# Summing the adaLN partial sums over the partitions on GpSimd instead of on the tensor engine

## The chip, the cores and the metric

The kernel runs on one core of a Trainium2 chip. The metric is the device time of one execution in microseconds, the median over several executions. Engine names are those of the profile: PE is the tensor engine (PEld its weight loads), DVE the vector engine, ACT the scalar engine, POOL is GpSimd, and SP is the queue that issues the loads.

## What is computed

The reference is two layers of a transformer-like block for 256 latent tokens and 256 context tokens of width 1024, in float32. Each layer has a mixer (two attentions and a pooling mixer in parallel, merged by gates) and a channel mixer (an MLP of width 4096). Both are modulated: a vector `c` per stream (one for the latents, one for the context) gives six rows of 1024 numbers per layer, a shift, a scale and a gate for each of the two sub-layers. The change touches the way in which these rows are computed.

```python
def adaln(v, w, b):
    m = jax.nn.silu(v) @ w + b
    return jnp.split(m, 6, axis=-1)

for l in range(DEPTH):
    sh1, sc1, g1, sh2, sc2, g2 = adaln(c, w_ada[l], b_ada[l])       # and the same with c_ctx
    h = rmsnorm(x, norm1[l]) * (1 + sc1) + sh1
    x = x + g1 * merge(...)(h)
    x = x + g2 * mlp(rmsnorm(x, norm2[l]) * (1 + sc2) + sh2, ...)
```

## The kernel before

The program is written out by cooperative threads under a planner (`_Flow`). Each engine has an estimate of its own time table (`_Engine`, line 78; PE in `_TensorEngine`), with a fixed cost and a cost per column for every instruction. A thread yields a time, an event or nothing, and the planner issues instructions in the order in which the engines should run them by these estimates. The order of every engine's queue is thus fixed when the program is built. On the chip each engine takes its queue in order and waits on semaphores where an input is late.

PE multiplies float32 values as pairs (a rounded part `hi` and a rest `lo`), three matmuls for each product (`mm3`, line 433). A weight piece of 128x1024 is loaded by SP into `st` (line 350), cast to `wh` by ACT and split into `wl` by DVE (`halves`, line 366). Four such pairs are in use at most (W_HL_BUFS), and loads run three pieces ahead.

The adaLN rows of the first norm of layer 0 are made on PE at the start (`First`, line 517). All others come later, beside the main work, in the thread `ada_all` (line 1757), at a low priority. For each half of a row (512 columns) `ada_acc` (line 564) loads the 1024x512 block of w_ada in four pieces and adds up silu(c) times the rows on DVE. The result is a tile `acc` of 128x512 for each stream, whose 128 partitions still have to be summed. There are 32 such tiles. They end in one of two ways:

- `ada_cols_end` (line 602), 20 tiles, for shift and scale. These are wanted as columns, with the features on the partitions. PE transposes the four 128x128 blocks into a PSUM bank, DVE reduces each block along its columns to one number a partition and adds the bias column. Both instructions are issued on DVE's queue in their planned order. When both of shift and scale are there, `finish_mod` makes the norm's factor. The tiles belong to norm 2 of layer 0 (8), norm 1 of layer 1 (8), norm 2 of layer 1 (4, the latents alone), in this order.
- `ada_rows_end` (line 637), 12 tiles, for the gates. These are wanted as rows on every partition. ACT and DVE split `acc` into a pair, PE multiplies it by a matrix that is filled with 0.5 or 1.0 (`ones`, lines 676 to 682), and DVE adds the bias row `grow`, which was loaded to all partitions. The factor 0.5 belongs to the first gate of each layer. The order is: first gate of layer 0 (4 tiles), second gate of layer 0 (4), first gate of layer 1 (2), second gate of layer 1 (2). `to_residual` (line 1479) multiplies the matmul's result by the row.

Both ends wait ADA_SLACK (10 us by the planner's clock, line 44) before the PE work, and take PSUM banks only where two stay free. `calm_way` (line 248) keeps this work away from the norms.

POOL does little: constants at the start, the power -1/2 in the norms (`norm_tile`, line 725) and in the normalisation of keys and queries (`qk_norm`, line 900, by `rms_scale`, line 706), the tables `tab`, and small memsets. For keys, DVE's product `z` reads the power's result at once.

Of the kernel before, what the change touches and what calls it, by code (L numbers as in the profile page):

```python
# [15 lines left out]
P = 128  # L16
# [15 lines left out]
B_BUFS = 64  # L32
# [11 lines left out]
ADA_SLACK = 10.0  # L44
# [7 lines left out]
# order in which the layers take the chunks of w_in (see _layout)  # L52
# [6 lines left out]
# the loads of the start: token tiles, halves of the first norm's shift and scale, halves of the first chunks  # L59
# [11 lines left out]
class _Event:  # L71
    """A point of the program whose results other threads wait for."""
# [5 lines left out]
class _Engine:  # L78
    """An engine whose instructions advance the flow's estimate of its time table."""
# [14 lines left out]
    def calm(self, slack):  # L94
        """wait until the engine's queue is short"""
        while self._end > self._f.now + slack:
            yield self._end - slack

    def __getattr__(self, op):
        fn = getattr(self._e, op)  # L100

        def call(*args, **kw):
# [9 lines left out]
            if kw.get("op") == ALU.pow:  # L112
                per, cost = 0.09, 0.37
            if self._sb and any(p.space == bass.MemoryType.SB for p in ins[:1]):
                cost += self._sb
# [22 lines left out]
class _TensorEngine:  # L138
# [6 lines left out]
    def _step(self, out, lhsT, rhs, size, transpose=False):  # L145
        """the array's clock is full in a tick after one with enough columns, else half"""
# [27 lines left out]
class _Flow:  # L174
    """Cooperative threads that emit the program in the order in which the tensor engine should run it.

    A thread yields None (it can go on at once), a time (it can go on then) or an event."""
# [26 lines left out]
    def ready(self, *aps, eng=None):  # L204
        """when an engine sees the last write to these regions"""
        got = 0.0
        for ap in aps:
            for b in self._blocks(ap):
                t, e, late = self.times.get(b, (0.0, None, 0.0))
                got = max(got, t if e is eng else t + late)  # L210
        return got
# [15 lines left out]
    def held(self, pool):  # L227
        """how many tiles of a pool are in use"""
        p = self.pools[pool]
        p[1] = [t for t in p[1] if t > self.now]  # L230
        return p[0] + len(p[1])

    def free(self, *aps):
        """the last uses of these tiles are in the program"""
# [8 lines left out]
    def room(self, pool, n, most):  # L243
        """wait until n more tiles of a pool fit"""
# [3 lines left out]
    def calm_way(self):  # L248
        """wait while any norm is on its way"""
# [39 lines left out]
# priorities of the threads, the lowest number first  # L289
# [4 lines left out]
def kernel(ctx: ExitStack, tc: tile.TileContext, a: dict, out: bass.AP):  # L294
# [55 lines left out]
    def stage(src, nk, ncol):  # L350
        """a load of at most 1024 columns, on its way"""
# [14 lines left out]
    def halves(v, nk, ncol):  # L366
        """(hi, lo) of a staged load's rows"""
# [13 lines left out]
    class Chunk:  # L381
        """the (hi, lo) pairs of a chunk's rows, in two pieces"""
# [12 lines left out]
        def used(self, k):  # L395
            """row k is not needed any more, nor are those before"""
# [3 lines left out]
    class Stream:  # L400
        """Chunks of weights [128, nk, ncol], each staged in two loads and split ahead of its use"""
# [24 lines left out]
        def next(self):  # L426
            """the next chunk"""
# [5 lines left out]
    def mm3(ps, lh, rh, start, stop):  # L433
        """ps (+)= (lh_hi + lh_lo)^T (rh_hi + rh_lo), without lo * lo"""
# [13 lines left out]
    class Pair:  # L448
        """a (hi, lo) pair of tiles that some thread is going to write"""
# [19 lines left out]
    def reload_x():  # L469
        """the stream's input for the first residual sum"""  # L470
# [14 lines left out]
    # silu(c) as columns: 0.5 c (1 + tanh(c / 2))  # L485
# [9 lines left out]
    # adds the (hi, lo) rows of both vectors  # L495
# [14 lines left out]
    def finish_mod(l, which, vec, half):  # L510
        """A = norm (1 + scale), B = shift as per-partition columns"""
# [5 lines left out]
    class First:  # L517
        """half of the columns of shift and scale of layer 0, norm 1, both vectors, on the tensor engine"""
# [6 lines left out]
        def row(self, typ, kk, w):  # L525
            """one of the eight row tiles of one type: rows (hi, lo) x vectors"""
# [37 lines left out]
    def ada_acc(l, j, vecs, accs):  # L564
        """per-partition partial sums of silu(c) @ w_ada[:, 512 j : 512 j + 512]"""
# [27 lines left out]
    def ada_cols(l, which, vecs):  # L593
        """shift and scale columns of norm `which`"""
# [6 lines left out]

    def ada_cols_end(l, which, vecs, half, typ, accs, left):
        idx = 3 * which + typ
        c0 = idx * 8 + half * 4
        yield fl.now + ADA_SLACK
        for acc, vec in zip(accs, vecs):
            yield from banks(1, 2)
            pt = bank("act")
            for i in range(4):
                PE.transpose(pt[:, i * P : (i + 1) * P], acc[:, i * P : (i + 1) * P], ident)  # L610
            yield fl.ready(pt)
            dst = mods[l][:, 2 * which + typ, vec, half * 4 : half * 4 + 4]
            V.tensor_reduce(out=dst, in_=pt.rearrange("p (i q) -> p i q", i=4), axis=AX.X, op=ALU.add)
            yield fl.ready(dst)
            V.tensor_tensor(out=dst, in0=dst, in1=b_col[:, l, c0 : c0 + 4], op=ALU.add)
            free(acc, pt)
# [12 lines left out]
    def ada_rows(l, idx, vecs, ones, factor):  # L629
        """factor * gate rows on every partition: rows[l, idx][vec][half]"""  # L630
        left = [0, 1]
        for half in range(2):
            accs = []
            yield from ada_acc(l, idx * 2 + half, vecs, accs)
            fl.spawn(ada_rows_end(l, idx, vecs, ones, factor, half, accs, left), P_ADA)

    def ada_rows_end(l, idx, vecs, ones, factor, half, accs, left):
# [8 lines left out]
        hl = []  # L646
        yield from fl.room("b", 2 * len(accs), B_BUFS - ADA_SPARE)
        for acc in accs:
            yield from fl.calm_way()
            ah, al = tmp(F32R, "ach"), tmp(F32R, "acl")  # L650
            yield from hilo_steps(acc, ah, al)
            hl.append((ah, al))
            free(acc)
        yield fl.ready(*[q for p in hl for q in p]) + ADA_SLACK
        for (ah, al), vec, g in zip(hl, vecs, gs):
            yield from banks(1, 2)
            ps = bank("ar")
            PE.matmul(ps, ones, ah, start=True, stop=False)
            PE.matmul(ps, ones, al, start=False, stop=True)
            free(ah, al)  # L660
            yield fl.ready(g, ps)
            yield from fl.calm_way()
            V.scalar_tensor_tensor(out=g, in0=g, scalar=factor, in1=ps, op0=ALU.mult, op1=ALU.add)
            free(ps)
# [9 lines left out]
    identr = const([P, P], F32R, "identr")  # L674
    S.copy(out=identr, in_=ident)
    ones = {}
    for f in (0.5, 1.0):
        of = half(s="ones")
        G.memset(of[:, :P], f)
        ones[f] = const([P, P], F32R, f"ones{f}")  # L680
        S.copy(out=ones[f], in_=of[:, :P])
        free(of)
# [23 lines left out]
    def rms_scale(ss, n, width):  # L706
        """(ss / width + eps) ** -0.5 in place"""
# [4 lines left out]
    class Normed:  # L712
        """hi and lo tiles of a modulated norm, features on partitions"""
# [11 lines left out]
    def norm_tile(l, which, t, xh):  # L725
        """x * rstd of one token tile"""
# [57 lines left out]
    def mod_out(l, which, hT, stream, k, v, cols, ev, by, ps, left):  # L784
        """a feature tile of the modulated norm"""
# [24 lines left out]
    def norm_by_tile(l, which, hT, t):  # L810
        """one token tile of the modulated norm of stream 0"""
# [36 lines left out]
    def layer(l, hT, hT_next):  # L848
# [6 lines left out]
        def pair(s):  # L855
            """(hi, lo) of NQ columns"""
# [5 lines left out]
        def duo(dt, s):  # L862
            """a tile of NQ columns"""
# [9 lines left out]
        # rope tables with the gains folded in: T[kind][:, 0] -> y0, T[kind][:, 1] -> y1  # L873
# [26 lines left out]
        def qk_norm(ps, c0, nh, kind, t, hi, lo, ev, rs=None):  # L900
            """heads ps[:, c0 : c0 + 64 nh], rotated, to hi and lo [P, nh, ..., 64]; normalised, or (queries) with the
            norm's factor times SCALE in rs"""
# [66 lines left out]
        def done_with(ps):  # L969
            """one of the threads that read this bank has read it"""  # L970
# [947 lines left out]
```

## Time and profile before

| | before |
|---|---|
| median of 3 executions | 1159.73 us (1159.59 to 1160.59) |
| the profiled execution, span from first to last instruction | 1159.7 us |
| mean granted clock of PE | 0.994 |
| busy: PE, DVE, ACT, POOL | 1138.5, 872.7, 636.2, 70.7 us |
| instructions: PE matmuls, DVE, ACT, POOL | 6636, 1653, 1356, 84 |

No time of the profiled execution other than its span is on the page; it agrees with the median to 0.1 us. Busy time counts an engine's own work. PE's matmuls overlap at their ends, so the start-to-start distance tells more of what one costs than its duration. The chain of the page follows the work that ended last backwards, and names for each step what it waited for.

### The profile page before, as it was taken

The numbers are of one execution on the slowest core, as the hardware profiler recorded it, in microseconds if no ns is written. First come the engines' busy times: TensorE is split into PE (matmuls) and PEld (weight loads), VectorE is DVE, ScalarE is ACT, GpSimd is POOL, SyncE is SP. The second block draws the span as 40 slices with busy tenths as digits, with TensorE's granted clock in tenths as the row PEclk, the third lists the DMA queues.
The fourth block names the chain that finished last, engine by engine and source line by source line (L and its number), as shares of the span: only waits on it lengthen the run. The fifth ranks groups of instructions, "written<-read, shape, count | busy, mean of one in ns | idle before, by whom it ended". The sixth has DMA issues, their size and how long they took to land.

```text
span 1159.7 us, 17946 instructions
## 1 busy us (share of the span) xinstructions
PE 1138.5 (98%) x6636; PEld 998.0 (86%) x6636; DVE 872.7 (75%) x1653; ACT 636.2 (55%) x1356; POOL 70.7 (6%) x84
## 2 busy tenths in 40 slices
PE   5999999999999999999999999989999999999998
PEld 2898889888888898888888888889999998999886
DVE  5878989889888679878677634689777885987453
ACT  6867786664633564321133323576877865666332
POOL 0224001100000000000000000023002000000000
PEclk9899999999999999999999999999999999999999
DMA  8752235243435435556655423554334471775562
GB/s 308 271 166 97 85 105 188 90 153 121 136 137 178 138 119 178 180 180 214 213 178 185 163 92 107 166 168 153 103 128 137 155 241 40 269 238 183 192 216 75
DMA packets 59992, 186.85 MB, mean 161 GB/s; under 512 B 7296, under 2 KB 8064, under 8 KB 59904
## 3 DMA queue, kind: packets, MB, share of 16 engines
q1 hardware_dynamic: 59904, 185.71, 47.8%
q8 instruction: 52, 0.85, 0.3%
q14 instruction: 36, 0.29, 0.1%
HBM read 184.63 MB, written 1.05 MB: 160 GB/s over the span
## 4 chain that ended last, share of the span: by engine, by line
PE 95%; DMA 2%; ACT 2%; DVE 1%; SPq 0%; issue 0%; POOL 0%; DVEq 0%; POOLq 0%
PE tm L167 28%; PE h L167 23%; PE g L167 17%; PE qkv L167 8%; PE br L167 6%; PE sc L167 3%; PE po L167 2%; PE pT L171 2%; PE u L167 1%; DMA ad<-in_wada_dram 1%; PE xT L171 1%; PE ada L167 1%; PE act L171 1%; PE qT L171 1%; PE kT L171 1%; ACT hh L133 1%
## 5 line engine op out<-in xcount | busy, mean ns | idle before, releaser
L133 DVE TENSOR_TENSOR wl<-st,wh 128x1024 fp32r<-128x1024 f32 x216 | 263.6, 1223 | 133.7 <-ACT wh L133 133.1
L133 ACT CAST wh<-st 128x1024 fp32r<-128x1024 f32 x216 | 227.9, 1058 | 231.8 <-PE tm L167 151.2
L167 PE MATMUL h<-hh,wh 128*128 128x256 f32 (+1 forms) x736 | 186.7, 316 | 0.0
L167 PE MATMUL h<-hh,wl 128*128 128x256 f32 (+1 forms) x512 | 168.8, 330 | 0.2 <-DVE wl L133 0.2
L133 DVE SCALAR_TENSOR_TENSOR acc<-sta,s_col,acc 128x512 f32<-128x512 f32 x224 | 159.3, 743 | 3.0 <-DMA sta<-in_wada_dram 2.4
L167 PE MATMUL tm<-wh,ah 128*128 128x512 f32 x384 | 150.3, 391 | 0.0
L167 PE MATMUL tm<-wl,ah 128*128 128x512 f32 x384 | 149.5, 389 | 0.0
L167 PE MATMUL tm<-wh,al 128*128 128x512 f32 x384 | 149.5, 389 | 0.0
L167 PE MATMUL g<-hh,wh 128*128 128x512 f32 (+1 forms) x384 | 132.6, 345 | 0.0
L167 PEld LDWEIGHTS h<-hh,wh 128*128 128x128 f32 x736 | 124.1, 190 | 8.8
L167 PE MATMUL g<-hl,wh 128*128 128x512 f32 (+1 forms) x384 | 129.3, 337 | 0.0
L167 PE MATMUL g<-hh,wl 128*128 128x512 f32 (+1 forms) x384 | 129.3, 337 | 0.0
L167 PE MATMUL h<-hl,wh 128*128 128x512 f32 (+1 forms) x288 | 105.4, 366 | 0.1
L167 PEld LDWEIGHTS h<-hh,wl 128*128 128x128 f32 x512 | 97.0, 190 | 9.3 <-DVE wl L133 0.5
L167 PEld LDWEIGHTS tm<-wh,al 128*128 128x128 f32 x384 | 72.1, 188 | 15.2
L167 PEld LDWEIGHTS tm<-wl,ah 128*128 128x128 f32 x384 | 72.1, 188 | 14.7
L167 PEld LDWEIGHTS tm<-wh,ah 128*128 128x128 f32 x384 | 72.1, 188 | 14.5
L167 PE MATMUL qkv<-wh,hh 128*128 128x256 f32 x272 | 79.7, 293 | 1.1 <-ACT hh L133 1.1
L167 PE MATMUL qkv<-wl,hh 128*128 128x256 f32 x272 | 79.0, 290 | 1.8 <-DVE wl L133 1.8
L167 PEld LDWEIGHTS g<-hh,wl 128*128 128x128 f32 x384 | 72.8, 190 | 8.0
L167 PE MATMUL qkv<-wh,hl 128*128 128x256 f32 x272 | 79.1, 291 | 0.1
L167 PEld LDWEIGHTS g<-hh,wh 128*128 128x128 f32 x384 | 72.8, 190 | 6.7 <-ACT p L133 0.3
(188 smaller groups left out, 2178.6 us busy)
## 6 DMA issues: line engine op xcount, KB each, us to landing
st<-in_w_dram SPq DMA_DIRECT2D x136, 512.0 KB, 4.5
sta<-in_wada_dram SPq DMA_DIRECT2D x80, 512.0 KB, 4.1
st<-in_win_dram SPq DMA_DIRECT2D x72, 512.0 KB, 4.6
ad<-in_wada_dram SPq DMA_DIRECT2D x32, 256.0 KB, 7.1
st<-in_wout_dram SPq DMA_DIRECT2D x8, 512.0 KB, 5.5
wor<-in_wout_dram SPq DMA_DIRECT2D x16, 256.0 KB, 4.9
grow<-in_b_ada_dram SPq DMA_DIRECT2D x12, 256.0 KB, 5.1
kr<-in_wbr_a_dram SPq DMA_DIRECT2D x12, 256.0 KB, 5.0
```

The lines of the kernel that those rows point to most:

```text
L133: return fn(*args, **kw)
L167: return self._e.matmul(out, lhsT, rhs, start=start, stop=stop)
L171: return self._e.transpose(out, in_, identity)
```

## The change

Each partial sum is added up over the partitions by one `partition_all_reduce` on POOL, which leaves the sum on every partition (`ada_sum`, new). For the gates POOL then adds the bias row. For shift and scale POOL multiplies the sum by the identity, block by block, into the tile of the partial sum, and DVE reduces the result along its columns as before, now from SBUF. The ones matrices, the splits of the gates' partial sums, the transposes and ADA_SLACK are gone. The factor 0.5 of the first gates moves into the residual's product. The planner books 0.4 us and 6.3 ns a column for the all-reduce. The rest of the diff takes out comments.

```diff
+from concourse.bass_isa import ReduceOp
...
-ADA_SLACK = 10.0
...
+            if op == "partition_all_reduce":
+                per, cost = 6.3e-3, 0.4
...
+    def ada_sum(acc):
+
+        yield fl.ready(acc)
+        yield from fl.calm_way()
+        yield from fl.room("b", 1, B_BUFS - ADA_SPARE)
+        tot = tmp(s="tot")
+        G.partition_all_reduce(tot, acc, P, ReduceOp.add)
+        yield fl.ready(tot)
+        return tot
+
     def ada_cols_end(l, which, vecs, half, typ, accs, left):
...
-        yield fl.now + ADA_SLACK
         for acc, vec in zip(accs, vecs):
-            yield from banks(1, 2)
-            pt = bank("act")
-            for i in range(4):
-                PE.transpose(pt[:, i * P : (i + 1) * P], acc[:, i * P : (i + 1) * P], ident)
-            yield fl.ready(pt)
+            tot = yield from ada_sum(acc)
+
+            dg = acc.rearrange("p (i q) -> p i q", i=4)
+            G.tensor_tensor(out=dg, in0=tot.rearrange("p (i q) -> p i q", i=4), in1=ident.unsqueeze(1).to_broadcast([P, 4, P]), op=ALU.mult)
+            free(tot)
+            yield fl.ready(acc)
+            yield from V.calm(ADA_CALM[l])
             dst = mods[l][:, 2 * which + typ, vec, half * 4 : half * 4 + 4]
-            V.tensor_reduce(out=dst, in_=pt.rearrange("p (i q) -> p i q", i=4), axis=AX.X, op=ALU.add)
+            V.tensor_reduce(out=dst, in_=dg, axis=AX.X, op=ALU.add)
...
-        hl = []
-        yield from fl.room("b", 2 * len(accs), B_BUFS - ADA_SPARE)
-        for acc in accs:
-            yield from fl.calm_way()
-            ah, al = tmp(F32R, "ach"), tmp(F32R, "acl")
-            yield from hilo_steps(acc, ah, al)
-            hl.append((ah, al))
+        for acc, vec, g in zip(accs, vecs, gs):
+            tot = yield from ada_sum(acc)
             free(acc)
-        yield fl.ready(*[q for p in hl for q in p]) + ADA_SLACK
-        for (ah, al), vec, g in zip(hl, vecs, gs):
-            yield from banks(1, 2)
-            ps = bank("ar")
-            PE.matmul(ps, ones, ah, start=True, stop=False)
-            PE.matmul(ps, ones, al, start=False, stop=True)
-            free(ah, al)
-            yield fl.ready(g, ps)
-            yield from fl.calm_way()
-            V.scalar_tensor_tensor(out=g, in0=g, scalar=factor, in1=ps, op0=ALU.mult, op1=ALU.add)
-            free(ps)
+            yield fl.ready(g)
+            G.tensor_tensor(out=g, in0=g, in1=tot, op=ALU.add)
+            free(tot)
             rows[l, idx][vec][half] = g
...
-                V.tensor_tensor(out=tm[:, c], in0=rows[l, idx][t // 2][n][:, c], in1=ps[:, c], op=ALU.mult)
+                row = rows[l, idx][t // 2][n][:, c]
+                if idx == 2:
+
+                    V.scalar_tensor_tensor(out=tm[:, c], in0=row, scalar=0.5, in1=ps[:, c], op0=ALU.mult, op1=ALU.mult)
+                else:
+                    V.tensor_tensor(out=tm[:, c], in0=row, in1=ps[:, c], op=ALU.mult)
```

## Rows read from the trace of the kernel before

**Rows 1.** The page, busy time of each engine, share of the span and instructions.
```profile
PE 1138.5 (98%) x6636; PEld 998.0 (86%) x6636; DVE 872.7 (75%) x1653; ACT 636.2 (55%) x1356; POOL 70.7 (6%) x84
```
**Rows 2.** The chain that ended last: its shares by engine, then by line.
```profile
PE 95%; DMA 2%; ACT 2%; DVE 1%; SPq 0%; issue 0%; POOL 0%; DVEq 0%; POOLq 0%
...
by line: PE tm L167 28.0%; PE h L167 22.6%; PE g L167 17.1%; PE qkv L167 7.7%; PE br L167 5.8%; PE sc L167 2.6%; PE po L167 2.4%; PE pT L171 2.2%; PE u L167 1.4%; DMA ad<-in_wada_dram 1.2%; PE xT L171 0.9%; PE ada L167 0.8%; PE act L171 0.8
```
**Rows 3.** Busy time by stage: us from:to, length, busy time (instructions), clock, DMA share, GB/s.
```profile
178.00:354.00 176.00, 176.00 (x980) 152.34 (x979) 152.25 (x326) 98.86 (x248) 7.96 (x8) 1.00 0.40 134
...
402.00:625.00 223.00, 222.92 (x1097) 188.09 (x1096) 176.43 (x266) 79.01 (x108) 2.94 (x2) 1.00 0.54 181
...
745.00:800.00 55.00, 51.92 (x362) 48.75 (x361) 45.41 (x117) 41.09 (x126) 18.55 (x20) 0.97 0.52 168
```
**Rows 4.** Tile act: count, ns min/median/max, first and last start us, forms.
```profile
L171 PE MATMUL act<-ident,acc x80: 270/272/273, 231.8 to 620.6; 128*128 128x128 f32 x80
L133 DVE TENSOR_REDUCE mod<-act x20: 673/682/687, 233.3 to 623.2; 128x4 f32<-128x512 f32 x20
```
**Rows 5.** Groups of instructions (busy us, mean ns, idle before); last, tile res (as rows 4).
```profile
L133 DVE SCALAR_TENSOR_TENSOR grow<-grow,ar 128x512 f32<-128x512 f32 x12 | 8.1, 676 | 0.0
L133 DVE TENSOR_TENSOR acl<-acc,ach 128x512 fp32r<-128x512 f32 x12 | 8.1, 678 | 0.0
...
L133 DVE TENSOR_TENSOR res<-grow,tm x33: 414/686/689, 362.6 to 1155.9; 128x512 f32<-128x512 f32 x31, 128x256 f32<-128x256 f32 x2
```
**Rows 6.** PE's timeline around one tile's transposes and one ones-matmul: start us, us, instruction.
```profile
231.78 0.60 PE L171 MATMUL act<-ident,acc 128*128 128x128 f32 x4
232.13 0.48 PE L167 MATMUL g<-hh,wh 128*128 128x512 f32 x1
232.45 0.40 PE L167 MATMUL g<-hl,wh 128*128 128x512 f32 x1
...
146.08 0.39 PE L167 MATMUL ar<-ach,ones0.5_108 128*128 128x512 f32 x1
146.31 0.39 PE L167 MATMUL ar<-acl,ones0.5_108 128*128 128x512 f32 x1
```
**Rows 7.** Groups of POOL's instructions, shapes kept apart.
```profile
L133 POOL TENSOR_TENSOR tab<-rope,gains 128x256 f32<-128x256 f32 x8 | 8.5, 1088 | 1.0 <-DMA gains<-in_gains_dram 1.0
```
**Rows 8.** POOL's timeline at the start of the kernel and of layer 1.
```profile
1.01 0.29 POOL masks.py:199 TENSOR_SCALAR_AFFINE_SELECT ident<-ident 128x128 f32<-128x128 f32 x1
1.39 0.19 POOL L133 TENSOR_TENSOR pair_sum<-ident 128x2 f32<-128x2 f32 x1
...
785.08 1.01 POOL L133 TENSOR_TENSOR rsqA<-rsqA,neg_half 128x4 f32<-128x4 f32 x1 [2.08 <-DVE y L133]
786.05 0.70 POOL L133 TENSOR_TENSOR qr<-qr,neg_half 128x2 f32<-128x2 f32 x1
```
**Rows 9.** ACT's table load; loads by size: count, KB each, us to landing.
```profile
L133 ACT ACT_TABLE_LOAD x1 | 1.3, 1283 | 0.7 <-PEq L1907 0.7
...
ad<-in_wada_dram SPq DMA_DIRECT2D x32, 256.0 KB, 7.1
...
sink<-in_sink_dram SPq DMA_DIRECT2D x1, 6.0 KB, 6.0
pscale<-in_pscale_dram SPq DMA_DIRECT2D x1, 2.0 KB, 5.4
```
**Rows 10.** DVE's timeline: partial sums that end, and the product of the keys.
```profile
121.98 1.40 DVE L133 SCALAR_TENSOR_TENSOR acc<-sta,s_col,acc 128x512 f32<-128x512 f32 x2
...
167.25 1.41 DVE L133 SCALAR_TENSOR_TENSOR acc<-sta,s_col,acc 128x512 f32<-128x512 f32 x2
...
180.56 0.29 DVE L133 TENSOR_TENSOR z<-qkv,qr 128x128 f32<-128x128 f32 x1 [0.68 <-POOL qr L133]
```
**Rows 11.** Tiles qr and wl, their durations as in rows 4.
```profile
L133 POOL TENSOR_TENSOR qr<-qr,neg_half x16: 695/698/1693, 64.8 to 862.3; 128x2 f32<-128x2 f32 x16
L133 DVE TENSOR_TENSOR wl<-st,wh x216: 1203/1224/1755, 24.5 to 1145.7; 128x1024 fp32r<-128x1024 f32 x108
```

More of the change, by code (lines that the diff above doesn't have):

```diff
@@ L604, in ada_cols_end @@
         c0 = idx * 8 + half * 4
-        yield fl.now + ADA_SLACK
         for acc, vec in zip(accs, vecs):
-            yield from banks(1, 2)
-            pt = bank("act")
-            for i in range(4):
-                PE.transpose(pt[:, i * P : (i + 1) * P], acc[:, i * P : (i + 1) * P], ident)
-            yield fl.ready(pt)
+            tot = yield from ada_sum(acc)
[4 more added lines that the diff above has]
+            yield from V.calm(ADA_CALM[l])
             dst = mods[l][:, 2 * which + typ, vec, half * 4 : half * 4 + 4]
-            V.tensor_reduce(out=dst, in_=pt.rearrange("p (i q) -> p i q", i=4), axis=AX.X, op=ALU.add)
+            V.tensor_reduce(out=dst, in_=dg, axis=AX.X, op=ALU.add)
             yield fl.ready(dst)
             V.tensor_tensor(out=dst, in0=dst, in1=b_col[:, l, c0 : c0 + 4], op=ALU.add)
-            free(acc, pt)
+            free(acc)
         left.pop()
@@ L627, with ada_rows @@
             rows_ev[l, i] = _Event()
-    def ada_rows(l, idx, vecs, ones, factor):
+    def ada_rows(l, idx, vecs):
         left = [0, 1]
@@ L634, in ada_rows, with ada_rows_end @@
             yield from ada_acc(l, idx * 2 + half, vecs, accs)
-            fl.spawn(ada_rows_end(l, idx, vecs, ones, factor, half, accs, left), P_ADA)
-    def ada_rows_end(l, idx, vecs, ones, factor, half, accs, left):
+            fl.spawn(ada_rows_end(l, idx, vecs, half, accs, left), P_ADA)
+    def ada_rows_end(l, idx, vecs, half, accs, left):
         yield from fl.room("grow", len(vecs), GROW_BUFS)
@@ L675 @@
     S.copy(out=identr, in_=ident)
[L676 to L682, printed above, removed]
     rope = const([P, 2, 2, HD], F32, "rope")
@@ L1758, in ada_all @@
         yield layer_started[0]
-        yield from ada_rows(0, 2, (0, 1), ones[0.5], 0.5)
+        yield from ada_rows(0, 2, (0, 1))
         yield from ada_cols(0, 1, (0, 1))
-        yield from ada_rows(0, 5, (0, 1), ones[1.0], 1.0)
+        yield from ada_rows(0, 5, (0, 1))
         yield from ada_cols(1, 0, (0, 1))
         yield from ada_cols(1, 1, (0,))
-        yield from ada_rows(1, 2, (0,), ones[0.5], 0.5)
+        yield from ada_rows(1, 2, (0,))
         yield mlp_started[1]
-        yield from ada_rows(1, 5, (0,), ones[1.0], 1.0)
+        yield from ada_rows(1, 5, (0,))
     layer_started = [_Event()]
```

## The prediction

> **What bounds the kernel now.** I read the page first, then the chain, the groups of instructions, the timelines of POOL, DVE and PE, and last the busy time by stage. The page says that the tensor engine sets the time: PE is busy for 1138.5 of 1159.7 us, DVE for 872.7 and POOL for 70.7 [rows 1]. The chain agrees: 95% of it is PE, and the transposes of the partial sums alone (PE act) stand in it with 0.8%, some 9 us [rows 2]. The profiled execution has a span of 1159.7 us; the median of the runs is 1159.73, so I sum against 1159.7 and add nothing.
>
> The engine next to PE is DVE, and its room differs by stage. From 178 to 354 us it is busy for 152.25 of 176, from 402 to 625 us for 176.43 of 223 [rows 3]. All 20 reduces of a partial sum into a column lie in these two stretches, 233.3 to 623.2 us [rows 4]. DVE also splits every weight piece (216 `wl`) and takes its instructions in order, so a DVE instruction that waits holds the weights back.
>
> **What goes.** On PE, 80 transposes and 24 ones-matmuls, two for each of the 12 `grow` [rows 4, 5]. Four transposes start at 231.78 and the second matmul behind them at 232.45, where a matmul alone takes 0.23 [rows 6]: 0.67 - 0.23 = 0.44 us a tile, times 20 is 8.8 us. A ones-matmul starts 0.23 us after the one before it [rows 6]: 24 x 0.23 = 5.6. Together 14.4 us, all of it on the bound. DVE loses 12 `acl` of 0.678 and 12 `grow` of 0.676, 16.2 us [rows 5]; ACT loses 12 casts `ach`. Both leave slack only. Gone as well are 32 uses of a PSUM bank and the 10 us of ADA_SLACK.
>
> **What costs nothing.** The halving moves into the residual: a SCALAR_TENSOR_TENSOR in place of a TENSOR_TENSOR, 0.676 (as `grow` has it) against 0.686 us at 128x512 [rows 5]. The 12 bias loads stay on SP's queue in number and size. The two ones tiles (two memsets, two casts) lie under the loads of the start.
>
> **What comes.** POOL gets 32 partition_all_reduce, 20 products with the identity and 12 adds. An elementwise pass over 128x256 takes 1.088 us there [rows 7], so one over 128x512 about 2. The all-reduce has no row. From below: one such pass, 2 us. From above: the dearest POOL work by column, the power, takes 1.01 us for four columns and 0.70 for two [rows 7, 8], 0.155 a column, 80 us for 512. I take 3.6, nearer to the lower end because the power computes much per element and a sum does not; it is also what the planner books (0.4 + 512 x 6.3 ns). In this sum its length delays nobody, since the planner places the readers behind it.
>
> The term that decides is one that the planner doesn't book: **the change of program on POOL**. The diff names the all-reduce's sum from another module (`ReduceOp` of `bass_isa`) than the ALU operations that POOL's other calls use. In the trace POOL goes from memset to select to elementwise in 0.4 us [rows 8], so those sit together. Nothing shows that the all-reduce sits with them. If it doesn't, each step from all-reduce to elementwise and back needs the other code first. Call the price s. Nearest rows: ACT's one table load, 1.28 us [rows 9], for the lower end; 7.1 us, the slowest kind of load [rows 9], twice (two fetches in a row) for the upper, 14.2. I take 7.1: code must come from memory, and even 2 and 6 KB took 5.4 and 6.0 us to land in the busy part [rows 9]. The Trainium skill's GPSIMD Engine Reference (Instruction dispatch) says that the first call to a freshly loaded POOL kernel pays about 6 us that no instruction in the profile shows. No row here shows it; by that figure, as an estimate, the sum below gives 1277 us.
>
> Who waits? In ada_cols_end each tile is an all-reduce and then a product on POOL, and then a reduce on DVE, which is issued when the planner holds the product done. The swap before the first all-reduce hides in POOL's idle time; the one before its product does not (s late), nor do the two of the second vector (2s). So 3s = 21.3 us of DVE standing still for a pair of tiles, s = 7.1 for a single one. Behind the reduce stand `wl` and the softmax's reduces.
> - 178 to 354 us: four pairs, 85.2 us. DVE has 176 - 152.25 = 23.75 free and gets 1.4 back; 60 us too many.
> - 402 to 625 us: four pairs and four singles, 113.6 us. Free 46.6, got back 5.4; 61.6 too many.
> - A power for layer 0's keys stands in POOL's queue behind the pair of tiles finished at 169, and DVE's `z` at 180.56 waited 0.68 for it [rows 10]; now 3s = 21.3 more.
> - 745 to 800 us: the two tiles of layer 1's first gate fall among a row of powers [rows 8]: 4s = 28.4, of which I take half, 14.2, for the path, since DVE is busy for 45.41 of 55 there [rows 3].
> - The second gate of layer 1 ends near 1050 and is first used after 1068: nothing.
> - Where DVE is the bound, PE's savings don't count. What counts are the 16 ones-matmuls outside 402 to 625 us: -3.7.
>
> Sum: 60 + 61.6 + 21.3 + 14.2 - 3.7 = 153.4; 1159.7 + 153.4 = **1313 us**. With every wait on PE's path at s = 7.1 it is 85.2 + 113.6 + 21.3 + 28.4 - 14.4 = 234, 1394 us; with s = 4 it is 23 + 12 + 12 + 8 - 3.7 = 51, 1211; with s = 10 and every wait exposed 1475. Below s = 2.4 or so the room on DVE takes the waits and the change wins.
>
> **Rivals.**
> 1. *No swap: the all-reduce is one more POOL operation.* Then the new POOL work (32 x 3.6 + 32 x 2 = 180 us) lies on an engine busy for 6%, and 14.4 us leave the bound: 1145 to 1150 us. For it: the chain, and POOL's idle time. Against: nothing here shows both kinds resident. Chance 0.11.
> 2. *The all-reduce itself is slow* and POOL becomes the bound: at the upper end, 32 x 80 = 2560 us. The sum crosses at some 8 us apiece, when DVE's waits use up its room; at 30 us, 28 tiles need 840 us where some 500 lie between the first finished sum at 123 [rows 10] and 625, and the kernel is near 1159.7 + 840 - 500 = 1500. For it: the power's price per column. Against: a sum is not a power. The Trainium skill's GPSIMD Engine Reference (Cross-partition — where GPSIMD wins) gives 247.7 us for a partition-axis reduce of 128x2048. By that, as an estimate, a tile takes 62 us and the kernel over 2000; it is another instruction, and no row here shows either. Chance 0.05.
> 3. *No swap, but POOL and DVE get in each other's way.* The power over two columns took 0.70 alone and 1.69 at worst where DVE was full, and `wl` 1.22 at the median and 1.76 at worst [rows 11]: they hinder each other somewhere. If DVE stood still for all of the new POOL work, 8 x 5.6 = 45 us against 25 free in the first stretch and 16 x 5.6 = 90 against 52 in the second give +20 + 38 - 3.7, 1214 us. Against: DVE's usual times beside POOL are the plain ones. Chance 0.04.
> 4. *The PE time saved turns into other waits*: no change. The chain has 95% PE, so hardly; 0.02.
>
> **How the numbers follow.** The forecast has the rest, 0.78, and its time is the sum, 1313. Its own range is s = 4 to s = 10 exposed, 1211 to 1475; I set 1210 to 1490, which also takes in rival 3 and part of 2, and leaves out rival 1 and the slower end of rival 2. Measurement tells 0.2%, 2.3 us, from no change. Faster 0.11 (rival 1), same 0.02, slower 0.87.
>
> **What would show it.** POOL's timeline: gaps of s between each all-reduce and the elementwise instruction behind it, with nothing in them. The waits: DVE `mod` <- POOL at the head of the list, with about 8 and 15 us for the tiles of a pair, and PE and ACT waiting on DVE `wl`. PE busy well under 98% from 178 to 625 us, unchanged after 800. The forecast is wrong if POOL goes from all-reduce to product within a microsecond: then rival 1, or 2 if the all-reduce's own record is tens of us long. If the gaps are there and the time is still under 1200, DVE's waits had more cover than its free time.

## The result, and the profile after

The changed kernel takes **1358.75 us** (median of 4 executions, 1356.91 to 1361.71) against 1159.66 us of the kernel before, run beside it: a ratio of 1.1717, 95% interval 1.1701 to 1.1734. It is 199 us slower. The forecast was 1313 us, with 1210 to 1490 for the range: right sign, in the range, 46 us low.

First the page of the changed kernel (it answers to [rows 1, 2]): busy time by engine, two of the sliced rows (busy tenths of PE, PE's granted clock) and the chain's shares.

```profile
PE 1167.8 (86%) x6532; PEld 1011.2 (75%) x6532; DVE 890.3 (66%) x1629; ACT 629.1 (46%) x1342; POOL 227.1 (17%) x146
...
PE   6999998588598999076478799999689999999998
...
PEclk8999999789798999678688899999989999999999
...
PE 60%; issue 13%; DVE 11%; POOL 7%; ACT 5%; DMA 3%; SPq 0%; POOLq 0%; DVEq 0%; ACTq 0%
```

No engine is full any more. PE has 104 instructions fewer and yet is busy for 29 us longer, because the clock that it was granted fell (0.928 on the mean, 0.994 before), and the chain has lost its 95% of PE to waits. POOL is at 17%, so it is not a matter of throughput. POOL's timeline around one pair of partial sums shows what fills the time:

```profile
226.37 3.25 POOL L135 PARTITION_ALL_REDUCE tot<-acc  x1 [6.02 <-PE g L169]
236.73 1.28 POOL L135 TENSOR_TENSOR acc<-tot,ident 128x512 f32<-128x512 f32 x1 [7.11 <-issue]
244.05 3.25 POOL L135 PARTITION_ALL_REDUCE tot<-acc  x1 [6.04 <-PE g L169]
254.22 1.25 POOL L135 TENSOR_TENSOR acc<-tot,ident 128x512 f32<-128x512 f32 x1 [6.93 <-issue]
```

Between an all-reduce and the product behind it lie 7.1 and 6.9 us, put down to "issue": nothing that the profile shows was waited for. On the way back it is 6.0 (the releaser named there, PE, is only the nearest event; the gap is as long wherever the pattern stands). DVE takes its reduces in order, so it stands for these gaps; the timeline of DVE for the same pair, and the list of waits:

```profile
238.04 0.69 DVE L135 TENSOR_REDUCE mod<-acc 128x4 f32<-128x512 f32 x1 [3.96 <-POOL acc L135]
...
255.51 0.69 DVE L135 TENSOR_REDUCE mod<-acc 128x4 f32<-128x512 f32 x1 [13.40 <-POOL acc L135]
```
```profile
DVE mod L135 <- POOL acc L135: 198.1, 19, 37.1
...
POOL acc L135 <- issue: 122.0, 17, 7.9
...
PE h L169 <- DVE wl L135: 52.0, 5, 40.3
...
PE tm L169 <- DVE wl L135: 45.3, 8, 14.5
...
DVE z L135 <- POOL qr L135: 31.8, 5, 15.7
```

The 20 reduces wait 198.1 us in all (times and longest follow the sum), and behind them the weight splits `wl`, for which PE waits.

Where in the kernel is the time? The table has the length of five stretches in the profiled execution of every version that was run: to the first matmul of w_out; from there to the first power of layer 0's second norm; layer 0's MLP, up to the first power of layer 1's first norm; layer 1's mixer, up to its second norm; the rest. The experiments are explained below.

| version | us | ratio (95%) | mixer 0 | w_out 0 | MLP 0 | mixer 1 | rest |
|---|---|---|---|---|---|---|---|
| before | 1159.7 | 1 | 354.3 | 32.6 | 350.8 | 225.4 | 196.7 |
| after | 1358.8 | 1.1717 (1.1701-1.1734) | 410.2 | 42.0 | 464.4 | 244.2 | 195.8 |
| no_swap | 1183.7 | 1.0192 (1.0172-1.0211) | 356.7 | 36.4 | 361.2 | 233.2 | 195.8 |
| planner_knows | 1319.4 | 1.1366 (1.1344-1.1388) | 374.1 | 35.4 | 467.9 | 243.1 | 196.3 |
| knows_late_free | 1201.3 | 1.0360 (1.0344-1.0376) | 372.4 | 34.8 | 347.2 | 246.1 | 195.8 |
| dve_product | 1182.0 | 1.0181 (1.0162-1.0200) | 354.5 | 32.6 | 345.4 | 250.1 | 195.8 |
| dve_knows | 1178.3 | 1.0140 (1.0114-1.0166) | 357.8 | 32.5 | 345.2 | 245.4 | 195.8 |
| dve_early | 1160.1 | 0.9997 (0.9988-1.0006) | 361.0 | 33.2 | 343.6 | 223.5 | 196.2 |
| cols_on_pool | 1302.1 | 1.1218 (1.1200-1.1235) | 399.8 | 47.1 | 428.2 | 225.3 | 196.7 |
| rows_on_pool | 1192.1 | 1.0272 (1.0257-1.0288) | 366.7 | 32.6 | 349.1 | 249.6 | 195.8 |
| before_pool_load | 1246.9 | 1.0744 (1.0725-1.0763) | 386.7 | 32.5 | 395.8 | 226.7 | 202.5 |
| before_swaps | 1217.3 | 1.0505 (1.0484-1.0526) | 366.9 | 34.4 | 374.9 | 244.0 | 200.7 |
| before_sums | 1205.5 | 1.0382 (1.0367-1.0398) | 372.4 | 32.6 | 370.8 | 226.9 | 200.8 |
| **hybrid** | **1154.5** | **0.9949 (0.9937-0.9962)** | 354.7 | 32.5 | 343.6 | 225.8 | 195.8 |

(Span of the profiled execution before: 1159.7; after: 1356.6; the stretches add up to the spans.) The change loses 55.9 us in mixer 0, 9.4 in w_out, 113.6 in MLP 0 and 18.8 in mixer 1. In the rest it gains 0.9.

### The profile page after: what moved, and what is told of

It is laid out like the page before. It is cut to its first block, busy times and chain, and to the rows that moved or that the text cites. A ratio compares the mean times of both kernels' runs of the same rounds, so it can differ in the third digit from the quotient of the medians.

```text
span 1356.6 us, 17962 instructions
## 1 busy us (share of the span) xinstructions
PE 1167.8 (86%) x6532; PEld 1011.2 (75%) x6532; DVE 890.3 (66%) x1629; ACT 629.1 (46%) x1342; POOL 227.1 (17%) x146
## 4 chain that ended last, share of the span: by engine, by line
PE 60%; issue 13%; DVE 11%; POOL 7%; ACT 5%; DMA 3%; SPq 0%; POOLq 0%; DVEq 0%; ACTq 0%
PE tm L169 17%; PE h L169 16%; PE g L169 10%; PE qkv L169 6%; POOL tot L135 4%; DVE acc L135 4%; PE br L169 3%; DVE wl L135 2%; PE sc L169 2%; POOL acc L135 2%; PE po L169 2%; PE pT L173 2%; DMA sta<-in_wada_dram 1%; ACT p L135 1%; DMA ad<-in_wada_dram 1%
## 5 line engine op out<-in xcount | busy, mean ns | idle before, releaser
L135 DVE TENSOR_TENSOR wl<-st,wh 128x1024 fp32r<-128x1024 f32 x216 | 268.6, 1248 | 107.3 <-ACT wh L135 105.9
L169 PE MATMUL h<-hh,wl 128*128 128x256 f32 (+1 forms) x512 | 172.7, 337 | 52.0 <-DVE wl L135 52.0
L169 PE MATMUL tm<-wl,ah 128*128 128x512 f32 x384 | 155.6, 405 | 45.3 <-DVE wl L135 45.3
L135 DVE SCALAR_TENSOR_TENSOR acc<-sta,s_col,acc 128x512 f32<-128x512 f32 x224 | 166.2, 776 | 7.8 <-DMA sta<-in_wada_dram 7.6
L135 POOL PARTITION_ALL_REDUCE tot<-acc x32 | 116.7, 3649 | 320.5 <-DVE acc L135 232.0
L169 PE MATMUL tm<-wh,al 128*128 128x512 f32 x384 | 154.2, 401 | 0.0
L169 PE MATMUL tm<-wh,ah 128*128 128x512 f32 x384 | 154.1, 401 | 0.0
L135 DVE TENSOR_REDUCE mod<-acc 128x4 f32<-128x512 f32 x20 | 13.7, 685 | 198.1 <-POOL acc L135 198.1
L169 PEld LDWEIGHTS tm<-wl,ah 128*128 128x128 f32 x384 | 75.3, 196 | 65.0 <-DVE wl L135 49.3
L169 PE MATMUL h<-hl,wh 128*128 128x512 f32 (+1 forms) x288 | 108.4, 376 | 0.1
L169 PEld LDWEIGHTS tm<-wh,ah 128*128 128x128 f32 x384 | 74.9, 195 | 16.2
```

The source lines that it names most:

```text
L135: return fn(*args, **kw)
L169: return self._e.matmul(out, lhsT, rhs, start=start, stop=stop)
```

## Experiments

**The gaps taken away (no_swap).** Three elementwise passes stand in for the all-reduce, so POOL never leaves its elementwise program. The sum over the partitions is left out.

```diff
-        G.partition_all_reduce(tot, acc, P, ReduceOp.add)
+        for _ in range(3):
+            G.tensor_tensor(out=tv, in0=av, in1=ident..., op=ALU.mult)
```

> The changed kernel with each all-reduce replaced by three elementwise passes of POOL over the same tile (1.27 us each, 3.8 in all, against 3.65), so the sum over the partitions is left out and all else stays: the waits, the order, the POOL time. Swap theory: POOL no longer changes its program, no gap of 6 to 7 us is left behind any instruction, the 198 us of DVE waiting for the product fall below 15, and the time is 1145 to 1153 us, below the kernel before. Contention theory (POOL and DVE hinder each other): POOL reads and writes at least as much as with the all-reduce, so the time stays over 1300 us.

Measured: 1183.7 us. Of the 199 us, 175 went when the all-reduces and with them the changes of program were gone, although POOL's busy time rose from 227.1 to 274.3 us. So the gaps, with what waits behind them, are the main cost, and not the time that POOL works. (That the all-reduce itself is cheap is seen in dve_early below, which has all 32.) But 24 us stayed where a gain was expected, and DVE is busy for 937.4 us against 872.7. Two groups of instructions of this kernel (busy us, mean ns of one, idle before it):

```profile
L135 DVE TENSOR_SCALAR acc<-sta,s_col 128x512 f32<-128x512 f32 x32 | 33.6, 1081 | 2.2 <-DMA sta<-in_wada_dram 2.2
...
L135 DVE TENSOR_REDUCE mod<-acc 128x4 f32<-128x512 f32 x20 | 13.6, 678 | 19.3 <-POOL acc L135 19.3
```

The reduces wait 19.3 us in place of 198.1. But the first pass over a partial sum, 479 ns a piece in the kernel before, takes 1081 here: DVE's operations on SBUF are drawn out while POOL works. That is rival 3's mechanism, to which two runs below come back.

**The planner told of the gaps (planner_knows, knows_late_free).** The planner adds 7 us whenever POOL's program changes, so that the readers are issued later. The second version also gives `tot` back to its pool only when its reader is done.

```diff
+            if self is f.pool and code is not None:
+                if code != f.code:
+                    self._end += 7.0
+                f.code = code
...
-            free(tot)
             yield fl.ready(acc)
+            free(tot)
```

> The changed kernel, and the planner books 7 us on POOL wherever an all-reduce follows an elementwise instruction or the other way round. The swaps themselves stay, some 60 of them. Swap theory: the price is in DVE's queue standing behind a product that is late, so with the readers issued later the waits of DVE for POOL fall from 198 us to under 40; what is left is the powers of the keys and of layer 1's start, which are planned late as well: 1150 to 1190 us. If the gaps or the POOL work cost by themselves (contention, memory traffic of the code), the time stays over 1300 us.

> The kernel whose planner books the swap, and the tile of the sum is handed back only when the planner holds POOL's product (or add) done, not when it is issued. Theory: with the swap booked POOL's queue is tens of us long, and a tile handed back at issue goes to ACT, which then waits for POOL; that was the wait of 71 us of ACT's relu for POOL, and PE's 72 and 38 us behind it. With the tile held longer these go, and the time falls from 1319 to 1180 to 1240 us. If it stays over 1300 us the waits come from POOL's work being too much, not from the tile.

Measured: planner_knows 1319.4 us, a miss. DVE's wait for `mod` fell from 198.1 to 57.9 us, but the list of waits has new entries:

```profile
PE tm L174 <- ACT ah L140: 72.0, 1, 72.0
...
ACT relu L140 <- POOL acc L140: 70.8, 1, 70.8
...
DVE mod L140 <- POOL acc L140: 57.9, 6, 18.1
```

One activation of ACT waits 70.8 us for a POOL product: the tile `tot` was given back when the product was issued, deep in POOL's queue, and ACT's `relu` was the next to get it. With the tile held to its reader's end (knows_late_free) that wait and DVE's for `mod` are gone, and the kernel takes 1201.3 us with the same all-reduces and products on POOL. The planner's order also has fewer changes of program: 42 in POOL's timeline, where the changed kernel has 62. These 42 changes and the new work on POOL together leave a loss of 41 us (the 64 changes of before_swaps below, 57). So most of the change's 199 us came from instructions that were queued in order before a late result.

**Product and addition on DVE (dve_product, dve_knows, dve_early).** POOL keeps the all-reduce, DVE multiplies by the identity and adds the bias. dve_knows adds the planner's 7 us. dve_early instead starts the gates' all-reduces before it waits for the bias tiles.

```diff
+            yield from V.calm(ADA_CALM[l])
-            G.tensor_tensor(out=dg, in0=tot..., in1=ident..., op=ALU.mult)
+            V.tensor_tensor(out=dg, in0=tot..., in1=ident..., op=ALU.mult)
...
-            G.tensor_tensor(out=g, in0=g, in1=tot, op=ALU.add)
+            V.tensor_tensor(out=g, in0=g, in1=tot, op=ALU.add)
```

> The changed kernel with the 20 products with the identity and the 12 adds of the bias on DVE instead of POOL; the all-reduces stay, the planner does not know of the swap. DVE gets 32 x 0.69 = 22 us, 6 more than the ones-matmuls' splits and adds had cost it. Swap theory: all-reduces now follow one another without a swap, and only powers between them need one: some 10 swaps instead of 60, at the keys near 180 us and at the start of layer 1, 5 to 20 us in all: 1150 to 1175 us. If the all-reduce itself hinders (its length, its port), 32 of them are still there and the time stays over 1250 us.

> Both edits: products and adds on DVE, and the planner books 7 us for each change of POOL's program. Swap theory: the few swaps left are planned for, 1145 to 1165 us, a few us under the run with the products alone on DVE. Contention theory: over 1250 us.

> The run with products and adds on DVE lost 25 us in one place, the mixer of layer 1 (250 us from its first power to the next norm's, 225 before), where the two all-reduces of layer 1's first gate stand among the powers because they wait for the bias tiles to come free. Here the gates' all-reduces no longer wait for the bias tiles: they run as soon as their sums are there, near 610 and 630 us, and only the adds wait. Swap theory: no change of program is left among the powers of layer 1, and the time is 1143 to 1158 us, the first version below the kernel before. If the all-reduces or the products on DVE cost by themselves, it stays over 1170 us.

Measured: 1182.0, 1178.3 and 1160.1 us, all three above their ranges, by 7, 13 and 2 us. Most of the change's loss is gone, though all 32 all-reduces are there. Without products and additions between them few changes of program are left: 11 in dve_product and dve_knows and 7 in dve_early, by POOL's timeline, against 62 in the changed kernel. Where dve_product loses the rest, the table tells: MLP 0 gains 5.4 us, mixer 1 loses 24.7. There the first gate's two all-reduces stand among the powers; the timeline of POOL:

```profile
775.98 2.26 POOL L135 TENSOR_TENSOR rsqA<-rsqA,neg_half 128x4 f32<-128x4 f32 x1 [12.43 <-DVE rsqA L135]
786.18 6.49 POOL L135 PARTITION_ALL_REDUCE tot<-acc  x2 [7.93 <-PE qkv L169]
800.47 1.05 POOL L135 TENSOR_TENSOR rsqA<-rsqA,neg_half 128x4 f32<-128x4 f32 x1 [7.81 <-issue]
```

22 us pass from the end of one power to the start of the next; before, the wait ahead of one was 2.08 [rows 8]. The planner's 7 us (dve_knows) change little about it, since they don't move the sums out of the powers' way. dve_early moves the two sums ahead, and mixer 1 has its 223.5 us. It is as fast as the kernel before: 7.2 us gained in MLP 0, 6.7 lost in mixer 0.

**Half of the change at a time (cols_on_pool, rows_on_pool).** In the first only shift and scale go over POOL, in the second only the gates; the other half is done as before on PE.

```diff
-            fl.spawn(ada_rows_end(l, idx, ...), P_ADA)
+            fl.spawn(pe_rows_end(l, idx, ...), P_ADA)
```

> Shift and scale columns as in the changed kernel (all-reduce and product on POOL, sum on DVE), gate rows as in the kernel before (ones-matmuls on PE). Theory (the loss is DVE standing in order before 20 reduces whose product is late on POOL): almost all of the loss stays, 1285 to 1330 us; DVE's waits at mod for POOL's acc 140 to 180 us, the rest of the 198 us gone because the one wait of 37 us stood behind the gate rows' all-reduces. Rival (every change of POOL's program costs, whoever waits): 40 of 64 changes are left and so 5/8 of 199 us, about 1285 us, with gate rows alone then at 3/8, about 1235 us.

> Gate rows as in the changed kernel (12 all-reduces and 12 additions on POOL), shift and scale columns as in the kernel before (transposes on PE, sum from PSUM on DVE). Theory: nothing on DVE waits in order for these additions, so almost nothing of the loss is left: 1155 to 1180 us, what is above 1160 standing in layer 1's mixer where the queries' powers queue behind all-reduces. Rival (every change of program costs alike): about 1235 us.

Measured: 1302.1 and 1192.1 us, losses of 142 and 32. A price for each change of program would give 125 and 75. The gates' half decides: its 32 us are far from 75 and agree with waiting in order, though they lie 12 us above what was expected. The waits for `mod` in cols_on_pool:

```profile
DVE mod L135 <- POOL acc L135: 167.9, 19, 15.4
```

The longest is 15.4 us, where the whole change has one of 37.1. The halves add up to 174 of 199 us. What is missing shows in MLP 0: +77.4 and -1.7 apart, +113.6 together. There the gates' four tiles stand right ahead of the next shift tile in POOL's queue, and DVE's first reduce waits for all of them; POOL, DVE and the busy time by stretch of the changed kernel (columns as in [rows 3]; the one before DMA share is the clock):

```profile
478.50 3.31 POOL L135 PARTITION_ALL_REDUCE tot<-acc  x1 [6.08 <-issue]
489.03 1.51 POOL L135 TENSOR_TENSOR grow<-grow,tot 128x512 f32<-128x512 f32 x1 [7.21 <-issue]
...
552.73 3.25 POOL L135 PARTITION_ALL_REDUCE tot<-acc  x1 [5.93 <-issue]
562.93 1.25 POOL L135 TENSOR_TENSOR acc<-tot,ident 128x512 f32<-128x512 f32 x1 [6.96 <-issue]
```
```profile
564.22 0.69 DVE L135 TENSOR_REDUCE mod<-acc 128x4 f32<-128x512 f32 x1 [37.07 <-POOL acc L135]
```
```profile
534.00:541.00 7.00, 7.00 (x33) 5.79 (x32) 0.00 (x0) 3.12 (x5) 3.25 (x1) 1.00 0.00 0
...
555.00:562.00 7.00, 0.00 (x0) 0.00 (x0) 0.00 (x0) 0.00 (x0) 0.97 (x1) 0.50 0.00 0
...
583.00:590.00 7.00, 3.84 (x9) 3.08 (x10) 7.00 (x11) 0.57 (x1) 0.00 (x0) 0.50 0.61 220
```

PE first lives on the weights already split, then stands; its clock goes from 1.00 (2.4 GHz) to 0.50 (1.2 GHz) in the idle stretch and is still 0.50 when it starts again.

The busy time of the kernel before and of cols_on_pool in mixer 0 (from 42 us on), w_out and MLP 0:

```profile
42.00:354.30 312.30, 312.30 (x1813) 273.22 (x1813) 269.80 (x605) 199.94 (x527) 33.67 (x37) 0.99 0.40 132
354.30:386.90 32.60, 32.60 (x145) 27.02 (x144) 24.54 (x40) 8.86 (x16) 0.05 (x1) 1.00 0.59 205
386.90:737.60 350.70, 350.38 (x1673) 294.03 (x1672) 242.97 (x352) 129.07 (x183) 4.01 (x4) 1.00 0.48 161
```
```profile
42.00:399.80 357.80, 318.08 (x1778) 275.59 (x1776) 272.25 (x591) 198.57 (x525) 72.33 (x52) 0.93 0.33 109
399.80:446.90 47.10, 38.37 (x145) 28.82 (x144) 35.24 (x57) 9.97 (x18) 1.31 (x2) 0.86 0.55 190
446.90:875.10 428.20, 367.01 (x1625) 301.89 (x1625) 249.59 (x348) 128.96 (x183) 66.43 (x28) 0.92 0.39 131
```

In rows_on_pool nothing on DVE waits for an addition, and MLP 0 loses nothing. Its 32 us stand in mixer 0 (+12.4: `z` waits 15.2 us for a key's power) and in mixer 1 (+24.2), both times a power behind an all-reduce. The wait in DVE's timeline:

```profile
195.29 0.29 DVE L135 TENSOR_TENSOR z<-qkv,qr 128x128 f32<-128x128 f32 x1 [15.22 <-POOL qr L135]
```

**What POOL's work costs by itself (before_pool_load, before_swaps, before_sums).** To the kernel before is added, for each of the 32 partial sums, work on POOL that nobody reads: four elementwise passes; an all-reduce and a product; an all-reduce alone. All else is the kernel before. The sources are constants, so POOL runs these pieces as early as its queue allows, often in a row.

```diff
+            G.partition_all_reduce(idle, icnt, P, ReduceOp.add)
+            G.tensor_tensor(out=idle, in0=idle, in1=ident..., op=ALU.mult)
```

> The kernel before, unchanged but for four elementwise passes of POOL over 128x512 that are put behind each of the 32 partial sums, 128 passes or some 165 us, whose result nobody reads and which wait for nothing but POOL. No program change. Contention theory: DVE's instructions with both inputs in SBUF get longer while POOL works, DVE's busy time grows by 30 to 60 us, and the time is 1165 to 1190 us although nobody waits for POOL's results. If POOL's work costs only those who wait for it, the time is 1159 to 1162.

> The kernel before, unchanged but for one all-reduce and one product of POOL behind each of the 32 partial sums, on a tile that nobody reads: all the program changes, no reader. Swap theory: POOL shows gaps of 6 to 7 us behind each, some 60 of them, but a swap costs only where something that DVE waits for stands behind it on POOL, which is the powers near 180 us and those at the start of layer 1: 1170 to 1215 us, against 1358 with the readers. If the swaps cost by themselves (the code's way through memory, DVE or ACT held up), the time is over 1300 us.

> The kernel before plus one all-reduce for each of the 32 partial sums into a tile that nobody reads, and no product. Theory (the all-reduce holds the path to SBUF that DVE's operations on two SBUF inputs need, so that DVE gets longer; and powers stand behind it where there are any): DVE's busy time grows by 10 to 40 us, some of its 128x512 additions last 2.7 us in place of 0.74, and the kernel takes 1165 to 1190 us. Rival (an all-reduce that nobody waits for costs nothing, and what the version without PE's work and with products on DVE lost was the products' own time): 1158 to 1163 us and no DVE instruction longer than before.

Measured: 1246.9, 1217.3 and 1205.5 us; all three lie above their ranges. In before_swaps the list of waits has the price of the gap, 448.0 / 64 = 7.0 us over both directions:

```profile
POOL idle L136 <- issue: 448.0, 64, 9.6
```

The products' gaps were 241.9 us for 32, 7.6 each, those ahead of the all-reduces 206.1 for 32, 6.4 each. With 448 us of gaps the version costs 57. DVE waits 47.5 us for powers of the norms that stand behind these pieces (6.3 before), and its busy time is 70 us longer, for the reason that the other two loads show. A gap that nobody queues behind is not seen to cost anything.

The dearest load is the one without any gap, before_pool_load, where DVE's busy time rose by 115 us to 987.8. before_sums shows the cause at its clearest: 14 all-reduces in a row on POOL (50.99 us, 3.64 each), what DVE did meanwhile, and the busy time in that stretch:

```profile
439.06 50.99 POOL L136 PARTITION_ALL_REDUCE idle<-icnt  x14 [6.09 <-issue]
```
```profile
442.51 3.39 DVE L136 SCALAR_TENSOR_TENSOR acc<-sta,s_col,acc 128x512 f32<-128x512 f32 x2
445.82 3.34 DVE L136 TENSOR_TENSOR acl<-acc,ach 128x512 fp32r<-128x512 f32 x2
449.09 0.68 DVE L136 TENSOR_TENSOR sq<-relu 128x512 f32<-128x512 f32 x1
449.69 3.39 DVE L136 SCALAR_TENSOR_TENSOR acc<-sta,s_col,acc 128x512 f32<-128x512 f32 x2
453.00 3.27 DVE L136 TENSOR_TENSOR wl<-st,wh 128x1024 fp32r<-128x1024 f32 x1
```
```profile
439.00:490.00 51.00, 43.69 (x237) 36.80 (x235) 50.81 (x34) 22.55 (x35) 49.73 (x14) 0.97 0.25 83
```

A `wl` takes 3.27 in place of 1.22 us; of two additions one takes some 2.7 and the other the usual 0.74. About one DVE instruction for each all-reduce is held for 2 us, and DVE gets 34 instructions done in 51 us while it counts as busy for 50.81. An operation that reads one of its inputs from PSUM is not held. Beside an earlier row of eight all-reduces (221.43 to 248.00 us) `th<-th,br` keeps its time, and of all 32 in this kernel none took more than 0.689 us:

```profile
231.34 0.68 DVE L136 SCALAR_TENSOR_TENSOR th<-th,br 128x512 f32<-128x512 f32 x1
```

The Trainium skill's page "SBUF — State Buffer" (section on the two separate sides) says that a DVE operation with two SBUF inputs and a POOL operation that reads SBUF share one pair of ports under an exclusive lock, held for a whole instruction. The runs agree on who is held, but not on how long: of the 3.3 to 3.6 us of an all-reduce some 2 are held (`wl` 3.27 - 1.22), and shorter DVE instructions pass in between.

**A version made to beat both (hybrid).** dve_early, but layer 0's mixer keeps PE's way for its gate and for norm 2, because there dve_early lost what it had gained. One ones matrix comes back.

```diff
+ (pe_cols_end if (l, which) in ((0, 1),) else ada_cols_end)(l, which, ...)
+ (pe_rows_end if (l, idx) in ((0, 2),) else ada_rows_end)(l, idx, ...)
```

> The version meant to beat both: layer 0's mixer keeps the kernel before's tensor-engine way (rows of gate 2 and columns of norm 2), everything after it takes the all-reduce with product and additions on DVE and the gates' all-reduces ahead of the wait for the bias tiles. By the all-DVE version's stages (6.8 us lost up to the w_out phase, 7.2 us gained in layer 0's MLP, 1.8 us gained in layer 1): 1150 to 1153 us, ratio about 0.993. If the port's contention follows the all-reduces wherever they stand: 1158 to 1162 us.

Measured: 1154.5 us, ratio 0.9949 (0.9937 to 0.9962), 5 us faster than before, and 1.5 us above the upper end of the first of the two expectations. Mixer 0 is within 0.4 us of before, MLP 0 7.2 us shorter, as in dve_early.

## Why the prediction was right, and where it was off

- **The price of a change of program.** Forecast 7.1 us, measured 6.0 (the pair shown) to 6.4 (mean of before_swaps) on the way to the all-reduce and 7.0 to 7.6 on the way back, in gaps with nothing in them, as "what would show it" said. The Trainium skill's GPSIMD Engine Reference (Instruction dispatch) has about 6 us for the first call to a freshly loaded kernel. The runs show a gap of that size not once but at all 64 changes of before_swaps. What POOL does in the gaps no trace here shows; the prediction took its price from the landing time of loads, and that it came so close may be luck. Rival 1 is out: an all-reduce does not sit with the elementwise program.
- **The all-reduce itself.** Forecast 3.6 us, measured 3.65, product 1.27 where about 2 was forecast. Rival 2 is out. The 62 us that the prediction estimated from the Trainium skill's GPSIMD Engine Reference (Cross-partition — where GPSIMD wins) belong to another instruction.
- **DVE's waits.** The forecast's two sums, 85.2 + 113.6 = 198.8 us, against 198.1 measured. That the totals agree is chance, for the parts do not: the seven waits up to 410 us come to 53.1, the other twelve to 145.0. A pair gave 6.5 to 17.4 us in the first stretch and 17.9 to 23.7 in the second (49.0 with the wait of 37.07) where 21.3 was forecast, a single tile 8.2 to 9.6 where 7.1 was.
- **First stretch and layer 0's keys.** Forecast 60 + 21.3 = 81.3, measured 55.9 + 9.4 = 65.3 up to the second norm. By the halves alone: shift and scale 45.5 + 14.5 = 60.0, the gates by the keys 12.4. That the 60.0 meet the forecast's 60 is chance too. DVE's waits of cols_on_pool up to the second norm are 57.7 us, where 85.2 were forecast, and PE stood for 48.4 of them (39.7 + 8.7), so DVE's room took up 9 and not 25; the other 11.6 us are PE's work at the lower clock (318.1 + 38.4 busy against 312.3 + 32.6).
- **Second stretch: the term that was mis-sized.** Forecast 61.6, measured 113.6. Alone, shift and scale lose 77.4 there: 61.2 us of it are idle PE (428.2 - 367.0), which is the forecast's term (12 waits of 110.2 us in all, forecast 113.6), and 16.6 are PE's own work at a mean clock of 0.92 (367.0 against 350.4 us busy before). The sum had no term for the clock. The other 36 us are put down to the gates' tiles ahead in POOL's queue: the wait of 37.07, which is 4.48 in cols_on_pool. The prediction asked what was queued behind a waiting DVE instruction, but for POOL's own queue only did so for the powers.
- **Layer 1's start.** Forecast 14.2, half of the possible 28.4; measured 18.8, and 24.2 with the gates alone. The mechanism was right, half was too little.
- **The sum and its range.** Against the forecast's terms the changed kernel lost 16.0 us less up to the second norm, 52.0 more in MLP 0, 4.6 more in mixer 1, and saved 0.9 behind it where 3.7 had been taken off: some 43 us in all, as the span of 1356.6 lies above 1313. So errors of both signs stand behind the 46 us by which the median was missed. The upper end has a slip: with s = 10 and every wait exposed the terms give 120 + 160 + 30 + 40 - 14.4 = 335.6, that is 1495 us; 1475 counts only half of layer 1's start.
- **PE's savings.** Where DVE has room they count in full: in MLP 0 dve_early gains 7.2 us, and the forecast's prices give 12 x 0.44 + 8 x 0.23 = 7.1. In mixer 0, where DVE has the least room, the same version lost 6.7 us, with DVE busy for 922.4 us in all in place of 872.7. This agrees with "where DVE is the bound, PE's savings don't count", but no run tests it alone.
- **Rival 3** was set aside because "DVE's usual times beside POOL are the plain ones". The rows before had too little POOL work to show it. It is real: about 2 us for each meeting with an all-reduce, about 1 with an elementwise pass (the longest `wl` of before_pool_load is 2.32 us). It accounts best for what no_swap, before_pool_load and before_sums lost. In the changed kernel it is the smaller part. DVE's busy time rose by 17.6 us although 16.2 us of its work are gone, so some 34 us were held; no_swap, with some 81 held (64.7 + 16.2), lost 24 us in all. How many of the 199 us it makes was not separated.

## What to carry to other kernels

Before a reduction goes to GpSimd, ask whether its instruction shares a program with the elementwise ones next to it: if not, every alternation costs 6 to 8 us here that no engine's busy time shows, and each reader queued in order pays it. Put the reader on another engine, or keep the foreign instructions together and away from what is urgent, and tell the planner the price; a pool tile must be held until its late reader is done. And work given to an idle POOL is not free for DVE: each 128x512 operation on SBUF there can hold one of DVE's, here by 1 to 2 us.

## What the runs showed of the hardware that was not expected

- An elementwise pass on POOL holds even tiny DVE operations, for most of its length. In before_pool_load, beside a row of 32 passes of 1.6 us each, the same operation on two columns took 1.27 and 0.21 us (DVE's timeline):

```profile
223.22 1.27 DVE L133 TENSOR_SCALAR neg<-neg,negsink 128x2 f32<-128x2 f32 x1
...
226.77 0.21 DVE L133 TENSOR_SCALAR neg<-neg,negsink 128x2 f32<-128x2 f32 x1
```

- The two directions of a program change differ: 7.6 us from all-reduce to elementwise and 6.4 back on the mean of before_swaps. Several all-reduces in a row pay once.
- Elementwise work whose result nobody reads can cost more than all-reduces with their gaps: 128 unread elementwise passes cost 87 us, 64 changes of program with 32 all-reduces and 32 products 57.
